# Hybrid token mixer on one core: state decay and scan products shared between VectorE and ScalarE, chunk norm column by column

## The chip, the core and the metric

The kernel runs on one core of a Trainium2 chip. A core has five engines that work side by side: TensorE (PE: matmuls, with weight loads listed as PEld), VectorE (DVE), ScalarE (ACT), GpSimd (POOL) and SyncE (SP, which here issues DMAs). Each engine works through its own instructions strictly in order, and waits for others by semaphores. SBUF is the on-chip memory that all of them read and write; PSUM receives TensorE's results.

The metric is device time in microseconds (us) of one execution. Before the change three runs took 1203.91, 1203.28 and 1203.84 us, with a median of 1203.84.

## The reference, cut to what matters

One layer: a token mixer with three parallel head groups (a state-space scan, SSD, in both directions; a Fourier mix; a pooling mix), whose outputs go through one output projection, and then a feed-forward part with a depthwise convolution. 1024 latent tokens of width 1024, and 256 context tokens from which the scan states start. The change lies in the scan and in the norm behind it:

```python
def ssd_chunked(X, dA, B, C, init_state):        # chunks of 128 tokens, 8 heads of 64 in 2 groups
    ...
    y_diag = jnp.einsum("bclhn,bcshn,bhcls,bcshp->bclhp", C, B, Lmat, X)
    decay_states = jnp.exp(A_cs[..., -1:] - A_cs)
    states = jnp.einsum("bclhn,bhcl,bclhp->bchpn", B, decay_states, X)
    ...
    new_states = jnp.einsum("bhzc,bchpn->bzhpn", chunk_decay, states)
    ...
    y_off = jnp.einsum("bclhn,bchpn,bhcl->bclhp", C, states, jnp.exp(A_cs))
    return (y_diag + y_off).reshape(b, L, h, p), final_state

def ssd_gate_norm(y, xs, z, d_skip, norm_w):
    y = (y + xs * d_skip[:, None]).reshape(bsz, L, SSD_WIDTH)
    y = (y * jax.nn.silu(z)).reshape(bsz, L, SSD_GROUPS, SSD_WIDTH // SSD_GROUPS)
    y = (y * lax.rsqrt(jnp.mean(y * y, -1, keepdims=True) + EPS)).reshape(bsz, L, SSD_WIDTH)
    return (y * norm_w).astype(z.dtype)
```

## The kernel before

The input projection leaves its columns in channel blocks; the last four of them are two Fourier blocks (pf0, pf1) and two pooling blocks (pp0, pp1). Each is a loop of 48 matmuls of 512 columns (`proj_feat`: 8 steps in the depth, each with weight block high and low part, as float32 products are made of rounded high and low halves). The scan is written as pieces (`mids`) into these loops, after every second step in depth, and runs while TensorE works on the projections.

**State steps.** `state_step(n, d)` carries the state of direction d (0 forward, 1 backward) over one chunk, seven steps each, 14 in all. GpSimd weights the chunk's inputs (`xweight`, L685, into `xw`, two buffers). Two matmuls (L710) leave the chunk's contribution in a PSUM tile `pst`. On VectorE L712 multiplies the old state (128 x 512: 2 groups x 4 heads x 64) with the decay of each head, `etot`, read by broadcast, and L715 adds `pst`; L717 writes the new state to DRAM. Steps 0 to 4 stand in the loop of pf1, steps 5 and 6 in that of pp0. In the same stretch stand the last masks of the scan (L645, L648 on ScalarE), the Fourier constants `cf` (L732/733, a DMA, and the matmuls pPQ, L738) and the Fourier fold of four blocks (L756 to L772).

**Scan chunks.** The chunks are taken in the order 4, 5, 6, 7, 3, 2, 1, 0. `Y(i)` calls the norm of the chunk before (`chunk_norm`), the products of the current one (`chunk_y`), and the transposes of the one before (`chunk_out`). In `chunk_y`:
- L900, GpSimd: y = skip x input, 128 x 512
- L908, TensorE: po = C x state, for each group a PSUM tile of 512 columns (2 directions x 4 heads x 64); L912: pd, eight products with the masks M
- L914, VectorE: t1 = po x `ecs` (one factor per row, direction and head, read by broadcast), one instruction of 128 x 512 per group. t1 has one buffer for all chunks
- L918: y += pd; L920, twice: y += one direction of t1; L921: y *= z, all on VectorE
- L924 to L928, ScalarE: the sum of squares of each group of 256, then Ln and Exp for a first reciprocal root

`chunk_norm` (L933 to L935) makes a Newton step on the two numbers of a row at once (`newton` with n = 2, four instructions, the last at L150) and multiplies y with the result by broadcast, 128 x 512. `chunk_out` transposes y in four blocks on TensorE (L940), and ScalarE copies them with a scale by column to yT (L944).

**Around them.** `wo_prep` loads a block of the output weights, multiplies it with the gate `g1b` (L975, on VectorE and GpSimd by turns) and splits it into a high part (L218, ScalarE) and a low part (L219). The first blocks' turns lie between the scan chunks; so do the pooling sums (L831 to L864) and the four-block Fourier products (L784, L787). Behind the scan stands the output projection (`out_tiles`, L1010).

**What sets the order.** The code is written stage by stage; a scheduler turns it into one instruction order for each engine, from its own costs of instructions and their dependencies. So an edit also moves instructions that it doesn't touch. Four PSUM tiles of 512 columns are shared in this stage by pst, pinit, po, pd, pyt and others.

## Time and profile before

| | |
|---|---|
| runs, median | 1203.91, 1203.28, 1203.84; 1203.84 us |
| profiled execution | 1204.77 us |
| its span | 1202.9 us |
| PE busy | 1129.9 us, 94% |
| PE weight loads | 918.1 us, 76% |
| DVE busy | 984.6 us, 82% |
| POOL busy | 609.5 us, 51% |
| ACT busy | 461.1 us, 38% |

The span runs from the first to the last instruction of the profiled execution; 1.9 us of its time lie around it. The shares are averages over stages with different limits: the input part up to some 230 us, the state steps and the scan chunks from about 241 to 398 us, and from there the output projection and the feed-forward part, which fill the rest. What the change touches lies in the middle stretch alone.

### The profile page before, as it was taken

To read this page: it belongs to the slowest core of one execution; us is meant where nothing else is said; L and a number is where in the kernel's file an instruction comes from. 1 tells how busy PE (TensorE), PEld (TensorE's weight loads), DVE (VectorE), ACT (ScalarE), POOL (GpSimd) and SP (SyncE) were. 2 spreads that over 40 slices of the span, in tenths; PEclk is the share of its full clock that TensorE was granted. 3 is DMA by queue.
4 is the path that set the end of the run, shared out by engine and by line. 5 is a ranking of instruction groups with operands and counts; after the bars stand their busy time and mean duration, and the time that the engine had idled before them with its cause. 6 is when DMAs were issued, how large, how long until landed. Compare 5 with 4: busy or idle time off the path is not lost.

```text
span 1202.9 us, 15202 instructions
## 1 busy us (share of the span) xinstructions
PE 1129.9 (94%) x5328; PEld 918.1 (76%) x5328; DVE 984.6 (82%) x1395; ACT 461.1 (38%) x790; POOL 609.5 (51%) x482
## 2 busy tenths in 40 slices
PE   4999999989878999899999999999999999999986
PEld 1698887777756787788888787888888888888864
DVE  4788787688899789799999968787777877777966
ACT  1273566721344232433232343333333334343553
POOL 0010122244254025664556477767676767676756
PEclk9999999999999999899999999999999999999988
DMA  9849465567524404223555346665556555555513
GB/s 309 283 163 324 128 213 167 170 195 221 189 89 166 148 35 141 97 88 108 172 166 176 118 154 219 192 199 175 182 183 190 193 192 190 188 184 184 197 40 140
DMA packets 151875, 206.48 MB, mean 172 GB/s; under 512 B 12253, under 2 KB 89067, under 8 KB 151799
## 3 DMA queue, kind: packets, MB, share of 16 engines
q1 hardware_dynamic: 151799, 205.51, 52.7%
q8 instruction: 42, 0.69, 0.2%
q14 instruction: 34, 0.28, 0.1%
HBM read 148.76 MB, written 56.71 MB: 171 GB/s over the span
## 4 chain that ended last, share of the span: by engine, by line
PE 69%; DVE 16%; DMA 6%; issue 3%; ACT 3%; POOL 2%; SPq 0%; DVEq 0%; ACTq 0%; POOLq 0%
PE pu L1353 22%; PE pdn L1187 16%; PE pu L1527 9%; PE pout L1010 4%; PE px L445 4%; PE pz L344 4%; PE pl L1584 3%; PE p L1353 3%; DMA bc<-cs_scratch 2%; DVE cv L1234 1%; PE pu L1245 1%; POOL cv L1224 1%; DMA xr<-in_x_dram 1%; DMA zb_r<-in_w_in_dram 1%; PE pm L298 1%
## 5 line engine op out<-in xcount | busy, mean ns | idle before, releaser
L1234 DVE SCALAR_TENSOR_TENSOR cv<-pu,ffc,cv 128x945 f32<-128x945 f32 (+6 forms) x362 | 425.6, 1180 | 74.1 <-ACT cv L1212 64.3
L1187 PE MATMUL pdn<-wd,gh 128*128 128x512 f32 x576 | 180.7, 395 | 0.3 <-DVE xt L1190 0.3
L1187 PEld LDWEIGHTS pdn<-wd,gh 128*128 128x128 f32 x576 | 108.2, 188 | 25.8 <-DVE xt L1190 1.0
L1187 PE MATMUL pdn<-wd,gl 128*128 128x512 f32 x288 | 113.6, 394 | 0.0
L1190 DVE TENSOR_TENSOR xt<-xt,pdn 128x512 f32<-128x512 f32 x128 | 87.4, 683 | 28.8 <-PE pdn L1187 24.4
L219 POOL TENSOR_TENSOR wul<-wur,wuh 128x1024 fp32r<-128x1024 f32 x29 | 72.3, 2495 | 39.3 <-ACT wuh L218 30.7
L1455 POOL TENSOR_TENSOR wdr<-wdr,g2b 128x512 f32<-128x512 f32 x44 | 57.4, 1309 | 54.7 <-DMA wdr<-in_ffn_w_down_dram 53.1
L219 POOL TENSOR_TENSOR S<-wur,S 128x384 fp32r<-128x384 f32 (+2 forms) x75 | 62.6, 861 | 36.8 <-ACT S L218 24.4
L1481 POOL TENSOR_TENSOR cv<-cv,cv 128x512 f32<-128x512 f32 x44 | 57.9, 1336 | 27.7 <-ACT cv L1480 27.7
L1212 ACT ACTIVATE cv<-pu,ffc 128x1024 f32<-128x1024 f32 (+3 forms) x46 | 53.4, 1164 | 43.5 <-PE pu L1353 21.5
L1353 PE MATMUL pu<-T,S 128*128 128x512 f32 x270 | 67.5, 393 | 0.4 <-POOL S L219 0.4
L644 POOL TENSOR_TENSOR bc<-bc,ncs 128x256 f32<-128x256 f32 x32 | 25.7, 807 | 76.4 <-DMA bc<-cs_scratch 62.1
L1187 PEld LDWEIGHTS pdn<-wd,gl 128*128 128x128 f32 x288 | 54.1, 188 | 12.8
L1480 ACT ACTIVATE cv<-cv 128x512 f32<-128x512 f32 x44 | 25.5, 625 | 90.9 <-DVE cv L1234 90.9
L1353 PEld LDWEIGHTS pu<-T,S 128*128 128x128 f32 x270 | 50.5, 188 | 12.8 <-POOL S L219 0.8
L1353 PE MATMUL pu<-h2h,wuh 128*128 128x512 f32 x150 | 59.1, 394 | 0.0
L206 POOL TENSOR_TENSOR h2l<-h2t,h2h 128x512 fp32r<-128x512 f32 x14 | 20.5, 1475 | 75.9 <-DVE h2h L205 75.9
L1353 PE MATMUL pu<-h2h,wul 128*128 128x512 f32 x150 | 59.0, 393 | 0.0
L1353 PE MATMUL pu<-h2l,wuh 128*128 128x512 f32 x150 | 58.5, 390 | 0.0
L219 POOL TENSOR_TENSOR gl<-cv,gh 128x512 fp32r<-128x512 f32 x44 | 56.7, 1309 | 1.5 <-PE pl L1584 0.7
L219 POOL TENSOR_TENSOR wd<-wdr,wd 128x512 fp32r<-128x512 f32 x42 | 53.8, 1303 | 4.7 <-ACT wd L218 4.6
L1527 PE MATMUL pu<-h2h,wuh 128*128 128x512 f32 x176 | 55.3, 395 | 0.0
(407 smaller groups left out, 2939.6 us busy)
## 6 DMA issues: line engine op xcount, KB each, us to landing
xt<-x_scratch SPq DMA_DIRECT2D x144, 256.0 KB
x_scratch<-xt SPq DMA_DIRECT2D x144, 256.0 KB
wur<-in_ffn_w_up_dram SPq DMA_DIRECT2D x44, 512.0 KB
wad<-in_w_ada_dram SPq DMA_DIRECT2D x32, 512.0 KB
wdr<-in_ffn_w_down_dram SPq DMA_DIRECT2D x44, 256.0 KB
wa<-in_w_ada_dram SPq DMA_DIRECT2D x32, 256.0 KB
bc<-cs_scratch SPq DMA_DIRECT2D x32, 256.0 KB
xr<-in_x_dram SPq DMA_DIRECT2D x8, 512.0 KB
```

Source lines behind the costliest of these rows:

```text
L219: return (eng or G).tensor_tensor(lo, raw, hi.bitcast(F32), op=ALU.subtract)
L344: TE.matmul(pt[:, j * 512 : j * 512 + ZW], a, b[:, k % 4, :], start=first and i == 0, stop=last and i == 2)
L445: TE.matmul(pt[:, q * 512 : q * 512 + 512], a[:, k, :], b[q][:, k, :], start=k == 0 and i == 0, stop=k == KD - 1 and i == 2)
L1010: TE.matmul(pt[:, nb * 512 : nb * 512 + 512], u, v[:, nb * 512 : nb * 512 + 512], start=first and i == 0, stop=last and i == 2)
L1187: TE.matmul(pt, u_, wd[nb][:, v_, :], start=i == 0, stop=i == n - 1)
L1190: V.tensor_tensor(xt, xt, pt, op=ALU.add)
L1212: tap[0] = S.activation(acc[:, a * 64 : b * 64], pt[:, a * 64 : b * 64], AF.Identity, bias=ffc[:, 396 + ct : 397 + ct], scale=factor(0, 0))
L1234: last = V.scalar_tensor_tensor(dst, pv[:, r0 + dy : r1 + dy, c0 + dx : c1 + dx], factor(dy, dx), dst, op0=ALU.mult, op1=ALU.add)
L1353: TE.matmul(dst, a[k][u], b[k][w], start=start and k == 0 and j == 0, stop=k == n - 1 and j == 2, skip_group_check=True)
L1455: G.tensor_tensor(raw, raw, g2b[:, s], op=ALU.mult)
L1481: G.tensor_tensor(acc[:, s], acc[:, s], acc_v[:, s], op=ALU.mult)
L1527: TE.matmul(pt[:, q * 512 : q * 512 + 512], a[:, k, :], b[q][:, k, :], start=k == 0 and j == 0, stop=k == KD - 1 and j == 2)
```

## The change

Three edits, all within the scan. What is computed stays the same.

- **Decay of the state.** The multiply of 128 x 512 on VectorE becomes one of 128 x 256 (group one); group two is done by four ScalarE instructions of 128 x 64, one for each head, with the factor of that head as a scale by row. The addition (now L717) waits for both.
- **Scan products.** Of the two multiplies of 128 x 512 in each chunk the second (group two) is replaced by eight ScalarE instructions of 128 x 64, one for each direction and head, that read po in PSUM and write t1. The additions (now L923) wait for both.
- **Chunk norm.** The Newton step is made for each of the two columns by itself (`newton` with n = 1, three instructions with a scalar by row, L141, L142, L144), and the multiply of 128 x 512 by broadcast becomes two of 128 x 256 with a scalar by row (L939).

GpSimd's sums of the blocks of h, and all else that GpSimd does, are the same before and after.

```diff
--- before.py
+++ after.py
@@ -709,9 +709,11 @@
         for g in range(2):
             TE.matmul(pt[:, g * 256 : g * 256 + 256], btok[g][:, ch, :], xw[:, g, :], start=True, stop=True)
         dst, src = qt(stag[d](), f"st{d}_{n + 1}", [P, 2, 256]), state[d]
-        V.tensor_tensor(dst[:].rearrange("p g (h q) -> p g h q", q=64),
-                                      src[:].rearrange("p g (h q) -> p g h q", q=64),
-                                      dv(etot, ch, d).unsqueeze(3).broadcast_to([P, 2, 4, 64]), op=ALU.mult)
+        V.tensor_tensor(dst[:, 0].rearrange("p (h q) -> p h q", q=64), src[:, 0].rearrange("p (h q) -> p h q", q=64),
+                        dv(etot, ch, d)[:, 0].unsqueeze(2).broadcast_to([P, 4, 64]), op=ALU.mult)
+        for h in range(4):
+            S.activation(dst[:, 1, h * 64 : h * 64 + 64], src[:, 1, h * 64 : h * 64 + 64], AF.Identity,
+                         scale=etot[:, ch, 8 + 4 * d + h : 9 + 4 * d + h])
         V.tensor_tensor(dst, dst, pt[:].rearrange("p (g n) -> p g n", g=2), op=ALU.add)
         state[d] = dst
         nc.sync.dma_start(ss[ch + 1 - 2 * d][:, d, :], dst[:].rearrange("p g n -> p (g n)"))
@@ -910,10 +912,11 @@
         pd = psb(f"pd{ch}")
         for i in range(8):
             TE.matmul(pd[:, i * 64 : i * 64 + 64], M[:, i, :], xt[:, i * 64 : i * 64 + 64], start=True, stop=True)
-        for g in range(2):
-            V.tensor_tensor(t1[:, g].rearrange("p d (h q) -> p (d h) q", q=64),
-                            pos[g][:].rearrange("p (a q) -> p a q", q=64),
-                            ecs[:, ch, g * 8 : g * 8 + 8].unsqueeze(2).broadcast_to([P, 8, 64]), op=ALU.mult)
+        V.tensor_tensor(t1[:, 0].rearrange("p d (h q) -> p (d h) q", q=64), pos[0][:].rearrange("p (a q) -> p a q", q=64),
+                        ecs[:, ch, 0:8].unsqueeze(2).broadcast_to([P, 8, 64]), op=ALU.mult)
+        for a in range(8):
+            S.activation(t1[:, 1, a // 4, (a % 4) * 64 : (a % 4) * 64 + 64], pos[1][:, a * 64 : a * 64 + 64], AF.Identity,
+                         scale=ecs[:, ch, 8 + a : 9 + a])
         yv = y[:].rearrange("p (g n) -> p g n", g=2)
         V.tensor_tensor(y, y, pd, op=ALU.add)
         for d in range(2):
@@ -931,8 +934,9 @@
     def chunk_norm(ch, y, yv, ssq, r):
         v = sm.tile([P, 2], F32, tag="sv", name=f"sv{ch}")
         V.tensor_scalar(v, ssq, 1.0 / 256.0, EPS, op0=ALU.mult, op1=ALU.add)
-        r = newton(r, v, 2, f"ssn{ch}")
-        V.tensor_tensor(yv, yv, r.unsqueeze(2).broadcast_to([P, 2, 256]), op=ALU.mult)
+        for g in range(2):
+            q = newton(r[:, g : g + 1], v[:, g : g + 1], 1, f"ssn{ch}{g}")
+            V.tensor_scalar(yv[:, g], yv[:, g], q, None, op0=ALU.mult)
 
     def chunk_out(ch, y, *_):
         py = psb(f"pyt{ch}")
```

Lines behind the edits shift by two to four: L715 becomes L717, L918 L921, L920 L923, L921 L924, L940 L944, L975 L979. ScalarE has 14 x 4 + 8 x 8 = 120 instructions more; VectorE has eight products fewer, and three instructions more in each of the eight norms. The order of the feed-forward part does not change. At three places it does in the stretch between.

**ScalarE, state steps.** st0_n and st1_n are the states of the two directions after n steps, pinit the first one, EU and bc parts of the scan's masks, wp0 and wp1 the weight blocks of pp0 and pp1, fu0 a copy of Fourier block pf0. Before:

```order
L645 ACTIVATE EU11_2429<-bc112_2436,ncs_1072 128x128 x2
L218 ACTIVATE wp0_h_2485<-wp0_r_2483 128x1024
L648 ACTIVATE EU11_2429<-EU11_2429 128x512
L752 COPY fu0_2463<-pf0_2308 128x512
L701 COPY st1_0_2419<-pinit1_2410 128x512
L645 ACTIVATE EU01_2551<-bc010_2552,ncs_1072 128x128 x2
L645 ACTIVATE EU01_2551<-bc012_2558,ncs_1072 128x128 x2
L648 ACTIVATE EU01_2551<-EU01_2551 128x512
L218 ACTIVATE wp1_h_2685<-wp1_r_2683 128x1024
```

After, from the same first state of direction 1:

```order
L701 COPY st1_0_2419<-pinit1_2410 128x512
L715 ACTIVATE st1_1_2463<-st1_0_2419,etot_1070 128x64 x4
L715 ACTIVATE st0_2_2527<-st0_1_2450,etot_1070 128x64 x4
L715 ACTIVATE st1_2_2540<-st1_1_2463,etot_1070 128x64 x4
L645 ACTIVATE EU01_2567<-bc010_2568,ncs_1072 128x128 x2
L645 ACTIVATE EU01_2567<-bc012_2574,ncs_1072 128x128 x2
L715 ACTIVATE st0_3_2588<-st0_2_2527,etot_1070 128x64 x2
L648 ACTIVATE EU01_2567<-EU01_2567 128x512
L715 ACTIVATE st0_3_2588<-st0_2_2527,etot_1070 128x64 x2
L715 ACTIVATE st0_4_2644<-st0_3_2588,etot_1070 128x64 x4
L715 ACTIVATE st1_3_2601<-st1_2_2540,etot_1070 128x64 x4
L218 ACTIVATE wp1_h_2725<-wp1_r_2723 128x1024
```

The decays of steps 1 to 4 now stand between the first state and the high part of wp1; the masks EU01 stand between those of steps 2 and 3, and the masks EU11, the high part of wp0 and the copy fu0 ahead of the first row shown.

**VectorE, from the last state step to the first scan chunk.** t1, po, pd, y and z are the tiles of chunk_y with the chunk's number; wor0 is the first block of output weights and g1b its gate. Before:

```order
L712 TENSOR_TENSOR st0_7_2737<-st0_6_2707,etot_1070 128x512
L712 TENSOR_TENSOR st1_7_2746<-st1_6_2716,etot_1070 128x512
L715 TENSOR_TENSOR st0_7_2737<-st0_7_2737,pst0_6_2734 128x512
L715 TENSOR_TENSOR st1_7_2746<-st1_7_2746,pst1_1_2743 128x512
L975 TENSOR_TENSOR wor0_3077<-wor0_3077,g1b_3075 128x1024
L914 TENSOR_TENSOR t1_4_2764<-po40_2765,ecs_1071 128x512
L914 TENSOR_TENSOR t1_4_2764<-po41_2768,ecs_1071 128x512
L918 TENSOR_TENSOR y4_2762<-y4_2762,pd4_2771 128x512
L920 TENSOR_TENSOR y4_2762<-y4_2762,t1_4_2764 128x512 x2
L918 TENSOR_TENSOR y5_2807<-y5_2807,pd5_2816 128x512
L921 TENSOR_TENSOR y4_2762<-y4_2762,z4_2655 128x512
```

After:

```order
L712 TENSOR_TENSOR st0_7_2785<-st0_6_2747,etot_1070 128x256
L712 TENSOR_TENSOR st1_7_2798<-st1_6_2760,etot_1070 128x256
L717 TENSOR_TENSOR st0_7_2785<-st0_7_2785,pst0_6_2782 128x512
L717 TENSOR_TENSOR st1_7_2798<-st1_7_2798,pst1_1_2795 128x512
L915 TENSOR_TENSOR t1_4_2820<-po40_2821,ecs_1071 128x512
L979 TENSOR_TENSOR wor0_3176<-wor0_3176,g1b_3174 128x1024
L921 TENSOR_TENSOR y4_2818<-y4_2818,pd4_2827 128x512
L923 TENSOR_TENSOR y4_2818<-y4_2818,t1_4_2820 128x512 x2
L924 TENSOR_TENSOR y4_2818<-y4_2818,z4_2695 128x512
```

The two decays are half as wide. One product of chunk 4 remains, and it stands ahead of the multiply of the weight block by the gate, no longer behind it; the chain of chunk 4 then runs through to the multiply by z, and the first addition of chunk 5 no longer stands in it.

**TensorE, where chunk 4 is transposed.** pp1 is the last pooling block, hl and hh the halves of the modulated input, pyt the transposed chunk, pft and pex the Fourier products, po60 and po61 the products of chunk 6. Before, after 34 of the 48 matmuls of pp1:

```order
L445 MATMUL pp1_2891<-hl0_193,wp1_h_2685 128x512
L445 MATMUL pp1_2891<-hl1_194,wp1_h_2685 128x512
L940 MATMUL pyt4_2837<-ident_75,y4_2762 128x128 x4
L784 MATMUL pft00_2870<-PQW_2585,f40_2469 128x128 x4
L784 MATMUL pft01_2876<-PQW_2585,f40_2469 128x128 x4
L787 MATMUL pex0_2882<-fex0_2478,PQW_2585 128x2
L908 MATMUL po60_2928<-S6_2794,cT6_1341 128x256 x2
L908 MATMUL po61_2931<-S6_2794,cT7_1540 128x256 x2
```

After, behind 8 of the 48:

```order
L445 MATMUL pp1_2966<-hh0_191,wp1_h_2725 128x512
L445 MATMUL pp1_2966<-hh1_192,wp1_h_2725 128x512
L944 MATMUL pyt4_2912<-ident_75,y4_2818 128x128 x2
L786 MATMUL pft00_2945<-PQW_2609,f40_2477 128x128 x4
L786 MATMUL pft01_2951<-PQW_2609,f40_2477 128x128
L944 MATMUL pyt4_2912<-ident_75,y4_2818 128x128 x2
L786 MATMUL pft01_2951<-PQW_2609,f40_2477 128x128 x3
L789 MATMUL pex0_2957<-fex0_2486,PQW_2609 128x2
L445 MATMUL pp1_2966<-hl0_193,wp1_h_2725 128x512
L445 MATMUL pp1_2966<-hl1_194,wp1_h_2725 128x512
```

The transposes of chunk 4 have moved ahead by 26 matmuls of pp1, and the Fourier products pft stand around them; those of chunk 6 have moved ahead by 10, behind the 24th.

On SP the DMA of the Fourier constants now stands ahead of the two state writes of step 2, the load of wor0 behind the state writes of step 1, and that of g1b between the two of step 7. On VectorE the low part of wp0 (L219) stood ahead of the first additions and now stands behind them, inside the Fourier fold (ahead of L773).

## Rows read from the trace of the kernel before

**Rows 1.** Busy time by stage, core 0; x counts instructions.

```profile
core 0: us, PE busy (x) PEld busy (x) DVE busy (x) ACT busy (x) POOL busy (x), PEclk, DMA share, GB/s
241.00:286.00 45.00, 39.90 (x172) 32.47 (x171) 41.65 (x79) 7.49 (x16) 24.93 (x23) 0.96 0.64 202
286.00:388.00 102.00, 83.34 (x427) 68.15 (x427) 90.28 (x143) 38.35 (x97) 41.20 (x20) 0.94 0.49 157
388.00:439.00 51.00, 51.00 (x219) 40.82 (x218) 39.30 (x99) 11.40 (x27) 0.00 (x0) 0.98 0.33 123
```

**Rows 2.** Waits of PE, 240 to 286 us: total us, times, longest.

```profile
PE pst L710 <- POOL xw L685: 2.6, 3, 1.1
PE pPQ L738 <- DMA cf<-in_fnet_w_dram: 2.5, 1, 2.5
```

**Rows 3.** Waits of PE, 286 to 390 us, the same columns.

```profile
PE pyt L940 <- DVE y L935: 6.2, 3, 3.0
PE ppool L871 <- DVE pT L864: 3.8, 1, 3.8
PE pyt L940 <- DVE s L863: 2.3, 1, 2.3
...
PE po L908 <- DVE t L914: 0.9, 1, 0.9
```

**Rows 4.** Groups of VectorE by shape, whole run: busy, mean ns | idle before.

```profile
L712 DVE TENSOR_TENSOR st<-st,etot 128x512 f32<-128x512 f32 x14 | 12.2, 882 | 0.1
...
L914 DVE TENSOR_TENSOR t<-po,ecs 128x512 f32<-128x512 f32 x16 | 10.5, 682 | 1.1 <-PE po L908 1.0
...
L150 DVE TENSOR_TENSOR ssn_q<-sr,ssn_t 128x2 f32<-128x2 f32 x8 | 6.7, 834 | 0.2
...
L320 DVE TENSOR_SCALAR xr<-xr,ln_mv,ln_q 128x1024 f32<-128x1024 f32 x6 | 4.6, 806 | 0.0
...
L141 DVE TENSOR_SCALAR pn_t<-pn_r,pn_v 128x1 f32<-128x1 f32 x16 | 4.3, 266 | 0.3
```

**Rows 5.** Timeline of VectorE: start, us, instruction, [idle before].

```profile
289.42 1.23 DVE L975 TENSOR_TENSOR wor<-wor,g1b 128x1024 f32<-128x1024 f32 x1 [3.40 <-DMA g1b<-ada_scratch]
290.57 1.28 DVE L914 TENSOR_TENSOR t<-po,ecs 128x512 f32<-128x512 f32 x2
...
292.48 0.94 DVE L920 TENSOR_TENSOR y<-y,t 128x512 f32<-128x512 f32 x1
...
302.84 2.32 DVE L150 TENSOR_TENSOR ssn_q<-sr,ssn_t 128x2 f32<-128x2 f32 x1
...
447.76 0.27 DVE L141 TENSOR_SCALAR pn_t<-pn_r,pn_v 128x1 f32<-128x1 f32 x1
...
448.26 0.21 DVE L144 TENSOR_SCALAR pn_q<-pn_t,pn_r 128x1 f32<-128x1 f32 x1
```

**Rows 6.** Group of ScalarE by shape, whole run.

```profile
L944 ACT ACTIVATE yT<-pyt,col 128x128 f32<-128x128 f32 x32 | 9.3, 367 | 22.8 <-PE pyt L940 22.8
```

**Rows 7.** Timeline of ScalarE in the scan stage.

```profile
296.62 1.06 ACT L218 ACTIVATE woh<-wor 128x1024 fp32r<-128x1024 f32 x1
...
297.77 0.99 ACT L831 COPY pT<-pp 128x1024 f32<-128x1024 f32 x1
...
307.82 1.14 ACT L944 ACTIVATE yT<-pyt,col 128x128 f32<-128x128 f32 x4 [4.87 <-PE pyt L940]
```

**Rows 8.** Timeline of TensorE, chunk 4.

```profile
287.55 1.90 PE L912 MATMUL pd<-xt,M 128*128 128x64 f32 x16
289.28 1.08 PE L908 MATMUL po<-S,cT 128*128 128x256 f32 x4
```

**Rows 9.** Timeline of GpSimd, three places.

```profile
289.53 3.33 POOL L975 TENSOR_TENSOR wor<-wor,g1b 128x1024 f32<-128x1024 f32 x1 [3.80 <-DMA g1b<-ada_scratch]
...
302.75 2.39 POOL L975 TENSOR_TENSOR wor<-wor,g1b 128x1024 f32<-128x1024 f32 x1 [9.89 <-DMA wor<-in_w_out_dram]
...
447.40 2.85 POOL L206 TENSOR_TENSOR h2l<-h2t,h2h 128x512 fp32r<-128x512 f32 x2 [1.50 <-DVE h2h L205]
```

## The prediction

> **What bounds the kernel now.** I looked first for the stretch in which the touched lines run (L712 from 241.9 us, L914 and L935 up to 398 us) and cut the run into stages there [rows 1]. From 241 to 286 us TensorE works 39.9 of 45 us, from 286 to 388 us only 83.3 of 102, and from 388 to 439 us all 51. So in the stage of the scan chunks TensorE stands idle 18.7 us, in the stage of the state steps 5.1 us, and behind 388 us it is the bound again. VectorE is busy 90.3 of 102 us and 41.7 of 45, ScalarE 38.4 and 7.5. A gain ahead of 388 us is kept behind it: the output projection runs without a gap, and the order of the feed-forward part does not change. Then I asked what ended TensorE's waits. In the state steps they are GpSimd's weighted inputs (2.6 us in three waits) and one DMA, that of the Fourier constants (2.5 us) [rows 2]. In the scan stage VectorE ends most [rows 3]: y of L935 6.2 us, pT 3.8, s 2.3 (this is the same wait for y, put down to its neighbour), t of L914 0.9. The kinds left out there end mostly on ScalarE and GpSimd. So 13.2 of the 18.7 us of idle end on VectorE. This is a stage bound by VectorE's chain from chunk to chunk, with ScalarE free for more than half of it.
>
> **Decay of the state (L712).** 14 multiplies of 128x512, 882 ns each on average [rows 4], become 128x256. An unhindered 512-wide one takes 0.68 us (L914), a 1024-wide one 1.23 (the first of [rows 5]), so 256 columns are worth 0.55 / 2 = 0.275 us: 14 x 0.275 = **3.9 us of VectorE**. Four ScalarE pieces of 128x64 with a scale by column replace them. The nearest row is L944, the same form at 128 columns out of PSUM: 0.367 us, four in 1.14, a pace of 0.26 [rows 6, 7]. Less 64 columns at 0.77 ns (from 0.367 at 128 columns to 1.06 at 1024 in the same rows) that is 0.32 us and a pace of 0.21; four take 0.95 us, 56 some 12 to 14 us. ScalarE has 37 us free there. What is new is a wait: L715 cannot add before ScalarE's four pieces, and on ScalarE the decays of step 4 stand behind the copy of wp1, which waits for TensorE. Behind a late L715 on VectorE wait the next steps and the fold; TensorE would wait if the PSUM tiles of pst came free late, and those are four steps ahead.
> Moved with it: the copy of wp0's low part leaves the place ahead of the first additions on VectorE, and on SP the Fourier constants go ahead of two state writes. Their DMA is issued once VectorE has merged the last masks, so a shorter VectorE chain brings it earlier. The most that can come of this stage is its 5.1 us of idle; the least is nothing, since 2.6 us end on GpSimd. Nothing says that all of either side is right, so I take half: **-2.5 us** (bounds 0 and -5.1; a loss is the second rival).
>
> **Scan products (L914).** Eight of 16 leave VectorE, each 0.60 us at its pace (two in 1.28, one 0.68 [rows 4, 5]): 8 x 0.60 = 4.8 us. Eight pieces on ScalarE per chunk take 0.32 + 7 x 0.21 = 1.8 us; they start when the product po of group two is done, and the products pd, which L918 needs first, then take another 1.73 us (1.90 with the overlap [rows 8]). So ScalarE's part is hidden as long as it starts at once. Not all 4.8 us are on the path. At 290.57 both L914 run while a GpSimd multiply is under way (289.53 to 292.86), and the sum L920 behind them, which reads SBUF twice, ends only 0.56 us after it [rows 5, 9]: one L914 less there gives nothing. By the timeline the second L914 of chunks 4, 7, 3 and 2 lies so beside GpSimd or ahead of a wait for TensorE or ScalarE, that of chunk 6 ahead of pd, that of chunk 0 behind 388 us. In the old order only chunks 5 and 1 gain: 1.2 us. In the new order VectorE has the first L914 ahead of the multiply that waits for g1b, and y4 is not woven into the pool sums any more, so more of it should count. Between 1.2 and 4.8 I take **-2.5 us**.
> The Trainium skill ("SBUF — State Buffer", section "Who interferes with whom") says that a VectorE instruction with two SBUF inputs contends with a GpSimd one that reads SBUF, and one with at most one SBUF input outside the two-port modes does not. Here the trace agrees (L914 ran on, L920 and L150 waited), and by that rule the products now moved held nothing that GpSimd wants; what it would make of the time is the first rival.
>
> **Norm by columns (L935).** One 128x512 multiply (0.68 us unhindered, as L914) becomes two of 128x256 with a scalar by row. TENSOR_SCALAR takes 0.27 us at one column (L141) and 0.81 at 1024 (L320), so 0.40 at 256 [rows 4]: two are 0.7 to 0.8 us. The Newton step goes from four small instructions to six, at most 2 x 0.2 us more: 8 x (0.1 + 0.4) = 4 us dearer at worst. Against it: L150 costs 6.7 us for eight results of two numbers [rows 4], since it waits for GpSimd (2.32 us at 302.84, ending with GpSimd's multiply [rows 5, 9]), whereas one-column steps run beside GpSimd (the three of 447.76 to 448.47 inside GpSimd's 447.40 to 450.25 [rows 5, 9]). The wait only moves to the multiply behind it, but the four or six steps are then done. I take **-0.5 us** (bounds +4 and -5).
>
> **The sum.** The profiled run took 1204.77 us, 0.93 above the median of 1203.84. -2.5 - 2.5 - 0.5 = -5.5 us, so 1199.3 in its own terms and **1198.3** by the median. TensorE's clock, granted at 0.94 and 0.96 in these stages against 0.98 behind them [rows 1], may give a little more where its waits go; I count it at nought.
>
> **Rivals.** *The shared reading of SBUF is the bound.* VectorE's two-input steps and GpSimd's steps exclude one another, and GpSimd is busy 41 of the 102 us [rows 1]. The moved products are not among those steps. Then stage one, whose waits end on GpSimd and a DMA, gives nothing, the scan stage the 1.2 us that the old order shows: 1204.77 - 1.2 - 0.93 = 1202.6, no change that can be measured. For it speaks [rows 5, 9]; against it that L712 is such a step and is halved, and L150 loses its wait.
> *ScalarE becomes the chain.* It works in order. In the scan stage the pieces of t stand in one queue with the copies of w_out (1.06 us) and pT (0.99 us) [rows 7]; if a chunk's pieces come behind both, they end 1.8 + 2.05 + 0.1 = 3.95 us after po instead of within pd's 1.73, so L920 starts 2.2 us late, once per chunk. Five of TensorE's waits end on a chunk's y or t: 5 x 2.2 = +11 us, with the -5.5 that makes 1203.84 + 5.5 = 1209.3. The single buffer of t1 adds to it: ScalarE can't write the next chunk's pieces until VectorE has read this one's. It decides once the delay exceeds 5.5 / 5 = 1.1 us per chunk. Against it: ScalarE is idle 64 of 102 us, and in the new order most groups of eight pieces stand ahead of the copies.
> *The whole chain comes loose.* y4 is transposed after 8 of the 48 products of pp1 instead of 34, so the waits of 2.3, 6.2 and 0.9 us in [rows 3] could go altogether, with the 2.5 us of the constants: -11.9 + 0.5, about 1192. Against it: TensorE now meets y4 earlier, and a late y4 stops it there with 40 products still to do.
>
> **How the numbers follow.** The forecast with its neighbourhood, 1195 to 1201.4: 0.40. The chain comes loose, below 1195: 0.17. SBUF is the bound, within 0.2% (1201.4 to 1206.2, about what a measurement of this kernel can tell from no change): 0.24. ScalarE is the chain, above 1206.2: 0.19. So faster 0.57, same 0.24, slower 0.19. The range goes from 1191, which cuts off perhaps 0.08 at the low end (the bounds -5.1 - 4.8 together with a gain in the norm), to 1207, half-way into the slower case, which leaves out about 0.12.
>
> **What would show it.** Right: TensorE idle in the state stage below 5 us, with its wait for the constants shorter, and in the scan stage below 16 us; the pieces at 0.3 us each; no wait of VectorE on ScalarE ahead of L920 or L715 longer than 0.5 us; the small steps of the norm without stalls of 2 us. Wrong: VectorE idle ahead of L920 or L715 for ScalarE (second rival); VectorE as long as before in steps of two SBUF inputs, with the stalls moved onto L935 and L920 (first rival); new waits of TensorE at the transposes of y, which now stand earlier. A difference behind 450 us would mean that the shift is not passed on, which I exclude here.

## The result and the profile after

Four runs of the changed kernel took 1195.23, 1194.09, 1193.51 and 1196.94 us, with a median of 1194.66; the kernel before has 1203.88 over four runs. The ratio is 0.9926 (95% interval 0.9909 to 0.9944): **8.9 us less, between 6.7 and 11.0**. The forecast was 1198.3, 5.5 less. The profiled execution took 1195.23 us, with a span of 1193.5.

The stages of [rows 1], after (the same columns):

```profile
241.00:286.00 45.00, 42.19 (x197) 34.31 (x196) 36.76 (x80) 23.53 (x79) 22.01 (x22) 1.00 0.66 217
286.00:388.00 102.00, 87.20 (x433) 71.97 (x432) 87.20 (x171) 53.79 (x168) 42.93 (x20) 0.92 0.51 175
388.00:439.00 51.00, 51.00 (x237) 41.10 (x236) 39.70 (x95) 13.12 (x26) 2.58 (x2) 1.00 0.21 76
```

TensorE idles 2.8 us where it idled 5.1, and 14.8 where it idled 18.7. VectorE is busy 4.9 and 3.1 us less, ScalarE 16.0 and 15.4 us more. The windows are the same clock times, but the changed kernel is up to some 4 us further on in its work; the stages further down are cut by the work instead. The waits of TensorE, from 240 to 286 us and from 286 to 390 us:

```profile
PE pst L710 <- POOL xw L685: 1.2, 2, 0.9
PE pst L710 <- DVE st L717: 0.9, 1, 0.9
PE pPQ L740 <- DMA cf<-in_fnet_w_dram: 0.6, 1, 0.6
```
```profile
PE ppool L873 <- DVE pT L866: 4.9, 1, 4.9
PE pyt L944 <- DVE y L939: 4.1, 2, 2.1
PE pyt L944 <- DVE ssn_q L144: 3.3, 1, 3.3
PE pout L1014 <- POOL yl L219: 1.6, 1, 1.6
PE po L910 <- ACT ft L787: 0.9, 1, 0.9
```

Against [rows 2] the wait for the Fourier constants fell from 2.5 to 0.6. Against [rows 3] the waits that end on y moved rather than went: one of 3.3 us now stands where chunk 4 is transposed. The groups of VectorE and ScalarE that the edits touch (form, count | busy, mean ns | idle before), to be laid beside [rows 4] and [rows 6]:

```profile
L923 DVE TENSOR_TENSOR y<-y,t 128x512 f32<-128x512 f32 x16 | 17.0, 1063 | 0.9
...
L712 DVE TENSOR_TENSOR st<-st,etot 128x256 f32<-128x256 f32 x14 | 8.3, 605 | 0.1
L939 DVE TENSOR_SCALAR y<-y,ssn_q 128x256 f32<-128x256 f32 x16 | 8.1, 532 | 0.0
...
L915 DVE TENSOR_TENSOR t<-po,ecs 128x512 f32<-128x512 f32 x8 | 5.5, 686 | 1.7 <-PE po L910 1.7
...
L141 DVE TENSOR_SCALAR ssn_t<-sr,sv 128x1 f32<-128x1 f32 x16 | 3.7, 267 | 1.2 <-ACT sr L931 1.2
...
L144 DVE TENSOR_SCALAR ssn_q<-ssn_t,sr 128x1 f32<-128x1 f32 x16 | 2.9, 207 | 0.0
...
L142 DVE TENSOR_SCALAR ssn_t<-ssn_t 128x1 f32<-128x1 f32 x16 | 2.2, 146 | 0.0
```
```profile
L715 ACT ACTIVATE st<-st,etot 128x64 f32<-128x64 f32 x56 | 15.0, 336 | 11.3 <-DVE st L717 10.3 <-DMA s_scratch<-st 0.6 <-DMA m_scratch<-EU 0.4
L918 ACT ACTIVATE t<-po,ecs 128x64 f32<-128x64 f32 x64 | 14.5, 328 | 18.2 <-PE po L910 9.6 <-DVE y L923 8.7
```

The sums of t (L923, before the change L920) were shorter before:

```profile
L920 DVE TENSOR_TENSOR y<-y,t 128x512 f32<-128x512 f32 x16 | 14.2, 889 | 0.3
```

**A ruler for all runs.** From TensorE's timeline I took four marks in each profile: the first matmul of the initial states, the first scan product, the products of the second pooling block (ppool, 359.49 us before), and the first matmul of the up-projection. Between them lie the state stage, the scan up to the pool, and the rest of the scan with the output projection. What follows the last mark took 735 to 738 us in every kernel, before and after alike; nothing was lost or won there. What lies ahead of the first mark took 235.6 to 239.9 us, though no edit touches it: that is how far one profile scatters.

| kernel | ratio of the times (95%) | state | to the pool | on to up | sum |
|---|---|---|---|---|---|
| before | 1 | 47.0 | 73.7 | 107.2 | 227.9 |
| all three edits | 0.9926 (0.9909 to 0.9944) | 43.5 | 69.5 | 107.4 | 220.4 |
| decay alone | 0.9982 (0.9968 to 0.9995) | 44.0 | 74.4 | 106.0 | 224.5 |
| products alone | 0.9949 (0.9931 to 0.9968) | 47.6 | 66.6 | 106.7 | 220.9 |
| norm alone | 0.9933 (0.9918 to 0.9949) | 45.5 | 69.1 | 104.0 | 218.7 |
| products and norm | 0.9951 (0.9935 to 0.9967) | 47.9 | 65.5 | 107.4 | 220.9 |
| decay and norm | 0.9935 (0.9912 to 0.9958) | 43.7 | 70.5 | 104.1 | 218.3 |
| order alone | 1.0004 (0.9990 to 1.0019) | 47.5 | 72.2 | 107.6 | 227.4 |
| products and norm, old order | 0.9983 (0.9969 to 0.9998) | 48.2 | 72.0 | 107.3 | 227.5 |
| all three, gate multiply later | 0.9945 (0.9924 to 0.9966) | 44.0 | 68.5 | 109.0 | 221.4 |
| before, gate multiply later | 0.9979 (0.9963 to 0.9994) | 47.1 | 67.6 | 107.6 | 222.3 |
| before, GpSimd's gate out | 0.9922 (0.9899 to 0.9945) | 47.4 | 70.0 | 101.2 | 218.6 |
| all three, GpSimd's gate out | 0.9879 (0.9855 to 0.9903) | 43.7 | 65.3 | 103.5 | 212.4 |
| all three, products' pieces twice | 0.9961 (0.9945 to 0.9976) | 44.5 | 73.8 | 104.9 | 223.2 |

The ratios are medians of 4 to 12 runs against before on the same chip; the stages are one profile each. Single executions of before went from 1196.7 to 1207.0 us in these comparisons, so a stage of one profile can be off by a few us and the ratios lead. The expectations quoted below count the stages a little otherwise (from the initial state of the second direction, 42.48 to 39.01 us; to the transposes behind the post-norm, 154.71 to 150.66, or 132.3 to 128.2 counted to the first of them); the differences, 3.5 and 4.05 us, are the same.

### The profile page after: what moved, and what is told of

Read it like the earlier page. It is cut to its first block, busy times and chain, and to the rows that moved or that the text cites. A ratio compares the mean times of both kernels' runs of the same rounds, so it can differ in the third digit from the quotient of the medians.

```text
span 1193.5 us, 15370 instructions
## 1 busy us (share of the span) xinstructions
PE 1125.1 (94%) x5328; PEld 914.8 (77%) x5328; DVE 971.3 (81%) x1411; ACT 488.9 (41%) x910; POOL 608.4 (51%) x482
## 4 chain that ended last, share of the span: by engine, by line
PE 55%; DVE 12%; DMA 4%; issue 3%; POOL 3%; ACT 1%; SPq 0%; DVEq 0%; ACTq 0%; POOLq 0%
PE pu L1357 21%; PE pdn L1191 14%; PE pu L1531 5%; PE pout L1014 4%; PE pl L1588 3%; PE p L1357 2%; DMA x_scratch<-xt 2%; DVE cv L1238 2%; PE pp L445 2%; PE pu L1249 1%; POOL cv L1228 1%; DVE y L923 1%; DVE xt L1194 1%; DVE T L219 1%; DVE xa L1084 1%
## 5 line engine op out<-in xcount | busy, mean ns | idle before, releaser
L219 POOL TENSOR_TENSOR wul<-wur,wuh 128x1024 fp32r<-128x1024 f32 x29 | 72.3, 2495 | 39.7 <-ACT wuh L218 39.7
L219 POOL TENSOR_TENSOR S<-wur,S 128x384 fp32r<-128x384 f32 (+2 forms) x75 | 62.1, 855 | 32.2 <-ACT S L218 24.3
L219 POOL TENSOR_TENSOR gl<-cv,gh 128x512 fp32r<-128x512 f32 x44 | 56.8, 1311 | 1.5 <-PE pl L1588 0.7
L219 POOL TENSOR_TENSOR wd<-wdr,wd 128x512 fp32r<-128x512 f32 x42 | 53.8, 1302 | 4.4 <-ACT wd L218 4.4
```

The costliest lines, as they stand in the source:

```text
L219: return (eng or G).tensor_tensor(lo, raw, hi.bitcast(F32), op=ALU.subtract)
```

## The experiments

### Each edit alone, and two together

The decay alone:

```diff
-        V.tensor_tensor(dst[:].rearrange(...), src[:].rearrange(...), ..., op=ALU.mult)
+        V.tensor_tensor(dst[:, 0].rearrange(...), src[:, 0].rearrange(...), ..., op=ALU.mult)
+        for h in range(4):
+            S.activation(dst[:, 1, ...], src[:, 1, ...], AF.Identity, scale=etot[...])
```

> Only the first edit: group two of the state's decay on ScalarE, scan products and norm as before. In the traces the stage from the first matmul of the initial states (L698) to the first scan product (L908) shrank from 42.48 to 39.01 us, the stage from there to the first transposes behind the post-norm (L189) from 154.71 to 150.66. Theory A, the parts act each in its own stage: the first stage is 3.5 us shorter here (39.0), the second one as before (154.7 within 0.5), the time 3.0 to 4.0 us below before. Theory B, the first stage gained only because the Fourier constants were issued earlier on SP (they stand ahead of the writes of step 2 here too): TensorE's wait for them falls from 2.5 to 0.6 us and its other waits in the stage stay as they were, so the gain is 2.0 us. Theory C, two-input reads of SBUF beside GpSimd are the bound: under 1 us.

Measured: 0.9982, 2.2 us less (0.6 to 3.8); the state stage 3.0 us shorter, the scan as before. TensorE's waits from 240 to 286 us:

```profile
PE pst L710 <- POOL xw L685: 2.0, 2, 1.6
PE pPQ L740 <- DMA cf<-in_fnet_w_dram: 0.8, 1, 0.8
PE pst L710 <- DVE st L717: 0.4, 1, 0.4
```

The wait for the constants gives 1.7 us, near the 1.9 of theory B, and the idle of the stage falls by as much (5.1 to 3.4 us). The other part of the 3.0 is TensorE's clock. In the profile of before the granted clock fell to the lower of its two levels, 1.2 instead of 2.4 GHz, behind the wait for the constants (windows of 3 us; PEclk is the third figure from the end):

```profile
260.00:263.00 3.00, 1.18 (x6) 0.70 (x4) 3.00 (x7) 0.63 (x1) 2.54 (x2) 1.00 0.96 234
263.00:266.00 3.00, 2.29 (x10) 2.22 (x11) 1.87 (x6) 0.00 (x0) 0.12 (x1) 0.64 0.63 238
266.00:269.00 3.00, 3.00 (x12) 2.40 (x11) 2.80 (x6) 0.20 (x1) 0.00 (x0) 0.79 0.32 87
```

0.36 and 0.21 of 3 us are 1.7 us, some of it while TensorE was idle; the matmuls of the whole stage were busy 41.9 us before and 40.7 with the decay on ScalarE, where the clock stays at 1.00. That is 1.3 us of the 3.0. The other profiles bear it out: in the six kernels with the new decay TensorE waited 0.6 to 0.9 us for the constants and the clock of the stage is 1.00; in seven of the eight with the old one it waited 2.5 to 3.5 us and the clock of the stage is 0.93 to 0.96. The eighth shows that the clock doesn't fall behind each such wait: with the norm alone TensorE waited 2.6 us at the same place and the clock stayed up (state stage 45.5).

The products alone:

```diff
-        for g in range(2):
-            V.tensor_tensor(t1[:, g]..., pos[g]..., ecs[...], op=ALU.mult)
+        V.tensor_tensor(t1[:, 0]..., pos[0]..., ecs[...], op=ALU.mult)
+        for a in range(8):
+            S.activation(t1[:, 1, ...], pos[1][...], AF.Identity, scale=ecs[...])
```

> Only the second edit: group two of the scan products on ScalarE; decay and norm as before. The transposes of chunk 4 stand after 13 of 48 matmuls of the last pooling block here (34 before, 8 with all three edits), the products of chunk 6 after 24 (34 before). Theory A, VectorE's chain is shorter by what leaves it: the stage from the first scan product to the post-norm transposes is 2.5 us shorter, and the time too; the other stage is as before. Theory B, the shared reading of SBUF is the bound, and the products are not among the steps that suffer from it: 1.2 us at most. Theory C, ScalarE's pieces come late: no gain or a loss, with VectorE waiting for ScalarE ahead of the additions of t. Theory D, it is the new order of TensorE that counts (chunk 6 is started 10 matmuls earlier): as much as with the norm alone, which has the same place for chunk 6.

Measured: 0.9949, 6.1 us less; all of it (7.0 us) between the first scan product and the pool. That is more than twice theory A's 2.5, and speaks against B and C. Seen from TensorE, 3.9 of the 7.0 us are less idle and 3.2 are shorter matmuls: its clock, 0.95 in this stretch before, is 0.98 here (the table under "What the waits for GpSimd cost").

The norm alone:

```diff
-        r = newton(r, v, 2, f"ssn{ch}")
-        V.tensor_tensor(yv, yv, r.unsqueeze(2).broadcast_to([P, 2, 256]), op=ALU.mult)
+        for g in range(2):
+            q = newton(r[:, g : g + 1], v[:, g : g + 1], 1, f"ssn{ch}{g}")
+            V.tensor_scalar(yv[:, g], yv[:, g], q, None, op0=ALU.mult)
```

> Only the third edit: the norm by columns; decay and products as before. The transposes of chunk 4 stand after 23 of 48 matmuls of the last pooling block, the products of chunk 6 after 24. Theory A (the prediction's term): 0.5 us less, bounds 5 less and 4 more; L150's 6.7 us are gone, but the wait has moved to the multiply behind it. Theory D, the order counts (chunk 6 started 10 matmuls earlier): as much as the products alone, 2 us or more.

Measured: 0.9933, 8.1 us less, as much as all three edits and far from theory A's 0.5. (Of the 9.2 us by which the stages of its profile are shorter, 1.5 lie in the state stage, which this edit doesn't touch.) Of before, L150 stands in [rows 4] with 6.7 us; its neighbours in the Newton step were not cheap either:

```profile
L146 DVE TENSOR_TENSOR ssn_t<-sr 128x2 f32<-128x2 f32 x8 | 3.4, 426 | 1.1 <-ACT sr L928 1.0
L147 DVE TENSOR_TENSOR ssn_t<-ssn_t,sv 128x2 f32<-128x2 f32 x8 | 2.9, 368 | 0.1
L148 DVE TENSOR_SCALAR ssn_t<-ssn_t 128x2 f32<-128x2 f32 x8 | 2.5, 309 | 0.1
```

Together the four took 6.7 + 3.4 + 2.9 + 2.5 = 15.5 us. With the norm alone:

```profile
L936 DVE TENSOR_SCALAR y<-y,ssn_q 128x256 f32<-128x256 f32 x16 | 11.6, 738 | 0.1
...
L141 DVE TENSOR_SCALAR ssn_t<-sr,sv 128x1 f32<-128x1 f32 x16 | 3.7, 265 | 0.8 <-ACT sr L928 0.8
L144 DVE TENSOR_SCALAR ssn_q<-ssn_t,sr 128x1 f32<-128x1 f32 x16 | 3.0, 205 | 0.0
...
L142 DVE TENSOR_SCALAR ssn_t<-ssn_t 128x1 f32<-128x1 f32 x16 | 2.2, 144 | 0.0
```

The six steps take 8.9 us in all eight chunks. The multiply rose from 7.6 us (L935 before, whole run) to 11.6: part of the wait did move there, but 6.6 went and 4.0 came. These 2.6 us alone don't make 8.1. Besides, y now becomes ready in halves: two of chunk 4's four transposes and the Fourier products run before the second half is there. What the halves are worth by themselves was not tested.

Products and norm together:

> Second and third edit together, the decay as before. The transposes of chunk 4 stand after 8 of 48 matmuls, as with all three edits. Theory A, the stages are independent: the first stage as before (42.5 us), the second as with all three (150.7), the time 4.0 us below before, and this gain and that of the decay alone add up to that of all three (9.2 by the medians, of which 1.6 lie ahead of and behind both stages in the traces and may not repeat). Theory D, the order makes the gain: no more than the better of the products alone and the norm alone.

Measured: 0.9951, 5.9 us less and no more than either alone. These two gains don't add up. The first stage is as before, and the stretch to the pool 65.5 us, not the 69.5 of all three edits as theory A has it. By the medians the decay's 2.2 us and these 5.9 do come to 8.1 of the 8.9 of all three; in the profiles the decay's gain is gone at the pool (state stage and stretch together 113.4 us here, 113.0 with all three). Theory D, that TensorE's new order makes the gain, fits so far: in all three kernels chunk 6 begins ten matmuls earlier than before.

Decay and norm, the products by the old code, completes the set:

> Decay and norm by the new code, the products by the old. Alone the decay gave 0.18% and the norm 0.67%, all three 0.74%. Theory P (parts add up): 0.85%, 10 us below before, faster than all three. Theory E (what the state stage gains ends at the gate's DMA, for which VectorE waits ahead of chunk 4's sums): VectorE's wait for it is 3.5 to 4 us instead of 3.0, the scan stage is 2 to 3 us longer than the 124.6 of the norm alone, and the time is that of the norm alone, 0.6 to 0.75%.

Measured: 0.9935, 7.8 us less, the time of the norm alone, as theory E has it; the interval just takes in the 0.9915 of theory P, so the time alone doesn't exclude that the parts add up. VectorE waits for the gate ahead of chunk 4's sums, a little less than the 3.5 to 4 us expected, and the scan stage is 1.4 us longer than with the norm alone (126.0), not 2 to 3:

```profile
286.96 1.23 DVE L978 TENSOR_TENSOR wor<-wor,g1b 128x1024 f32<-128x1024 f32 x1 [3.35 <-DMA g1b<-ada_scratch]
```

### Order without work, work without order

The kernel before, with the matmuls of pp1 behind the 24th issued behind the transposes of chunk 5:

```diff
+                    with tc.issue_after(anchor[0].ins) if anchor[0] is not None else ExitStack():
                         TE.matmul(pt[:, q * 512 : q * 512 + 512], a[:, k, :], b[q][:, k, :], ...)
...
-    p1 = proj_p(1, wnext, [[], [Y(2)], [], [Y(3)]])
+    p1 = proj_p(1, wnext, [[], [Y(2), hold], [], [Y(3)]])      # hold: anchor[0] = last transpose
```

> The kernel before with none of the three edits; only TensorE's order is changed: the matmuls of the last pooling block behind its 24th are issued behind the transposes of chunk 5, so that chunk 4 is transposed after 24 of them and chunk 6 begins there (34 and 34 before). The scan stage, counted here from the first scan product to the first transposes behind the post-norm, took 132.3 us before, 124.7 with the products alone, 124.6 with the norm alone, 124.3 with both, 128.2 with all three edits. Theory D, the place of chunk 6 in TensorE's order is what shortened it: 124 to 126 us here, the time 6 to 8 us below before. Theory A, the work that left VectorE shortened it: no gain, since VectorE has all of it here; the transposes of chunk 4 wait 2 to 4 us longer, 132 us or more.

Measured: 1.0004, no gain. Theory D, that the order alone does it, falls: TensorE meets chunk 4 earlier, and waits for it (its waits from 286 to 390 us; the wait is put down to a neighbour of y in VectorE's queue):

```profile
PE ppool L875 <- DVE pT L868: 5.6, 1, 5.6
PE pyt L944 <- DVE s L867: 4.5, 1, 4.5
```

Products and norm, with chunk 4's transposes, the first Fourier products and chunk 6 held behind the 36th matmul:

```diff
-    four_chan(0, *f0)
...
-    p1 = proj_p(1, wnext, [[], [Y(2)], [], [Y(3)]])
+    p1 = proj_p(1, wnext, [[], [], [out4, Y(2)], [Y(3)]])      # out4: chunk_out(4), four_chan(0)
```

> Products and norm by the new code, decay by the old one, but TensorE's order held near that of before: chunk 4 is transposed, the first Fourier products are made and chunk 6 begins behind the 36th of 48 matmuls of the last pooling block (34 before; with the same two edits and the scheduler's own order 8 and 24). Theory D (order): the gain is lost, the scan stage is 131 to 133 us (before 132.3, the same two edits in their own order 124.3). Theory A (work that left VectorE): most of the gain stays, 127 us or less.

Measured: 0.9983, 2.0 us of the 5.9. So neither theory holds by itself: less work on VectorE is worth 2 us while TensorE keeps its old order, the new order is worth nothing while VectorE has its old work, and together they are worth some 6.

### The gate's DMA ahead of chunk 4

With all three edits VectorE's timeline reads (start, us, instruction, [idle before]):

```profile
282.83 0.69 DVE L915 TENSOR_TENSOR t<-po,ecs 128x512 f32<-128x512 f32 x1 [0.55 <-PE po L910]
287.21 1.22 DVE L979 TENSOR_TENSOR wor<-wor,g1b 128x1024 f32<-128x1024 f32 x1 [3.69 <-DMA g1b<-ada_scratch]
288.35 0.68 DVE L921 TENSOR_TENSOR y<-y,pd 128x512 f32<-128x512 f32 x1
289.14 2.90 DVE L923 TENSOR_TENSOR y<-y,t 128x512 f32<-128x512 f32 x2
```

The scan stage begins 4.05 us earlier than before (281.77 against 285.82), but the gate lands only 2.2 us earlier (287.21 against 289.42, [rows 5]), and VectorE stands still for it with chunk 4's products waiting. TensorE then waits, and its clock falls behind the wait (the transposes of chunk 4; windows of 3 us):

```profile
296.91 0.45 PE L944 MATMUL pyt<-ident,y 128*128 128x128 f32 x1 [3.32 <-DVE ssn_q L144]
```
```profile
293.00:296.00 3.00, 0.58 (x3) 0.15 (x1) 3.00 (x11) 3.00 (x13) 0.00 (x0) 0.99 0.28 86
296.00:299.00 3.00, 2.09 (x10) 2.12 (x11) 2.97 (x6) 2.09 (x7) 0.00 (x0) 0.50 0.15 16
299.00:302.00 3.00, 3.00 (x15) 2.96 (x14) 1.13 (x6) 2.29 (x6) 1.04 (x1) 0.50 0.22 76
302.00:305.00 3.00, 3.00 (x13) 2.42 (x12) 3.00 (x12) 0.03 (x1) 0.00 (x0) 0.87 0.01 3
```

The lower level takes up to (0.50 + 0.50 + 0.13) x 3 = 3.4 us there. The kernel before loses as much elsewhere in this stretch (granted clock 0.95 in both), the products and the norm without the decay next to nothing (0.99): the same matmuls are busy 58.7 us with all three edits and 56.6 with those two. Would it help to issue that multiply behind chunk 4?

```diff
+        with tc.issue_after(gated[4].ins) if i == 0 else ExitStack():      # gated[4]: y4 *= z4
-        (G if i % 2 else V).tensor_tensor(raw, raw, g1b[0], op=ALU.mult)
+            (G if i % 2 else V).tensor_tensor(raw, raw, g1b[0], op=ALU.mult)
```

> All three edits; on VectorE the multiply of the first output weight block by the gate is issued behind chunk 4's multiply by z, no longer ahead of its additions. With all three edits VectorE waits 3.69 us there for the gate's DMA, chunk 4 is transposed late (TensorE waits 3.3 us) and the granted clock is at half for some 6 us behind it. Theory E, this wait eats what the state's decay gained: the wait at the transposes of chunk 4 goes, the clock does not fall there, the scan stage is 122 to 125 us instead of 128.2 and the time 4 to 6 us below that of all three edits (1194.7). Theory F, the decay's ScalarE pieces or the DMAs are what costs the 4 us: the stage stays at 127 to 129.

> The kernel before with none of the three edits; on VectorE the multiply of the first output weight block by the gate (3.40 us of wait for the gate's DMA ahead of it) is issued behind chunk 4's multiply by z. The scheduler then transposes chunk 4 after 18 of 48 matmuls of the last pooling block and begins chunk 6 after 24. Theory D (order): a scan stage of 123 to 126 us and a time 6 to 9 us below before, as the products or the norm alone bring. Theory A (work that left VectorE): only the wait counts, 1 to 3 us below before.

Measured: 0.9945 with all three edits (not better than 0.9926, the intervals overlap) and 0.9979 without them, 2.5 us less, which is A's 1 to 3 and not D's 6 to 9. With all three edits the first half of theory E came true: chunk 4 is transposed 13.5 us behind the first scan product instead of 15.1, TensorE's wait there is 1.2 us instead of 3.3, the clock doesn't fall behind it, and chunk 6 begins 19.2 us behind the first scan product instead of 24.1. The second half didn't: the scan stage takes 128.8 us, a length that theory F had named, though VectorE doesn't wait for ScalarE's pieces in this trace. VectorE's sums of chunk 4 (L923) now start at 284.10 and take 3.54 us, because GpSimd's multiply by the gate begins beside them. VectorE's and GpSimd's timelines, and the group of the pooling results:

```profile
284.10 3.54 DVE L923 TENSOR_TENSOR y<-y,t 128x512 f32<-128x512 f32 x2
```
```profile
284.74 2.35 POOL L980 TENSOR_TENSOR wor<-wor,g1b 128x1024 f32<-128x1024 f32 x1 [6.43 <-DMA g1b<-ada_scratch]
```
```profile
L862 DVE SCALAR_TENSOR_TENSOR pT<-s,pe,pT 64x1008 f32<-64x1008 f32 x4 | 9.1, 2284 | 0.1
```

Those four took 5.0 us before (1259 ns each) and 7.0 with all three edits (1761), and TensorE's wait for the second pooling block is 6.6 us instead of 4.9. VectorE's stalls beside GpSimd up to that place grew by 3.6 us (11.3 to 14.9, the table below), about as much as the 3.7 us saved at the gate.

### What the waits for GpSimd cost

To see their price, GpSimd's four multiplies by the gate were left out (10.9 us of GpSimd in the trace of before; those weight blocks are then not gated), before and after:

```diff
-        (G if i % 2 else V).tensor_tensor(raw, raw, g1b[0], op=ALU.mult)
+        if i % 2 == 0:
+            V.tensor_tensor(raw, raw, g1b[0], op=ALU.mult)
```

> The kernel before, but the four multiplies of an output weight block by the gate that are GpSimd's are left out (those blocks are not gated). Two of them lie in the stretch from the first scan product to the products of the second pooling block (73.7 us before, 69.1 with the norm alone, 69.5 with all three edits), 3.33 and 2.39 us long; VectorE's result of two numbers (L150) took 2.32 us beside the second. TensorE's order stays. Theory G (VectorE's steps that read SBUF twice wait for GpSimd, and the chain passes that on): L150 takes under 0.3 us at that place, chunk 4 is transposed some 2 us earlier, the stretch is 2 to 4 us shorter. Theory N (the stalls lie beside other waits): the stretch is as long within 1 us.

> All three edits, GpSimd's four multiplies by the gate left out as in the other kernel of this kind. With all three edits the sums of t (L923) took 2.90 us for two beside the first multiply and 2.75 beside the second, 1.3 us unhindered. Theory G: they take 1.3 to 1.6 us there, chunk 4 is transposed 1.5 us earlier, TensorE's wait of 3.3 us shrinks by as much, and the stretch to the products of the second pooling block is 2 to 4 us shorter than 69.5. Theory N: within 1 us of it.

Measured: 0.9922 and 0.9879, that is 9.4 us below before, and some 5.7 below all three edits (0.9926 - 0.9879, two comparisons). VectorE at the two places (the first line without the edits, where [rows 5] has 2.32 us; the second with them, where 2.90 stood):

```profile
300.20 0.16 DVE L150 TENSOR_TENSOR ssn_q<-sr,ssn_t 128x2 f32<-128x2 f32 x1
```
```profile
288.76 1.49 DVE L923 TENSOR_TENSOR y<-y,t 128x512 f32<-128x512 f32 x2
```

Theory G holds: the stretch to the pool is 3.7 and 4.2 us shorter with TensorE's order unchanged, chunk 4 is transposed 2.9 and 1.5 us earlier. That much is shown. With all three edits 2.7 of the 4.2 us are busy time of TensorE (58.7 to 56.1): it waits 1.8 us for chunk 4 instead of 3.3, and its clock stays at 1.00 throughout. Not all of the 9.4 us need be contention: without the multiply the weight blocks are also ready sooner for the splits and the output projection, which gained 6.0 us; the two weren't separated.

For the whole stretch the stalls can be counted from VectorE's timeline. For each instruction from the first scan product to the pool I took its time less the shortest that the same operation and shape took there in any of these runs, where that is over 0.15 us. Every instruction so counted overlaps one of GpSimd. Beside it stands TensorE in the same stretch (one profile each; us, and the granted clock):

| kernel | stretch | TensorE busy | TensorE idle | clock | VectorE's stalls |
|---|---|---|---|---|---|
| before | 73.7 | 59.9 | 13.8 | 0.95 | 15.0 |
| decay alone | 74.4 | 61.1 | 13.4 | 0.93 | 15.6 |
| products alone | 66.6 | 56.7 | 9.9 | 0.98 | 11.9 |
| norm alone | 69.1 | 56.8 | 12.3 | 0.96 | 11.8 |
| products and norm | 65.5 | 56.6 | 9.0 | 0.99 | 12.2 |
| decay and norm | 70.5 | 56.9 | 13.7 | 0.99 | 12.0 |
| all three edits | 69.5 | 58.7 | 10.7 | 0.95 | 11.3 |
| order alone | 72.2 | 59.2 | 13.1 | 0.94 | 10.7 |
| products and norm, old order | 72.0 | 60.5 | 11.5 | 0.92 | 17.0 |
| all three, gate multiply later | 68.5 | 57.9 | 10.5 | 0.95 | 14.9 |
| before, GpSimd's gate out | 69.9 | 61.1 | 8.9 | 0.93 | 13.1 |
| all three, GpSimd's gate out | 65.3 | 56.1 | 9.2 | 1.00 | 7.9 |

TensorE does the same matmuls in every row; what differs in its busy time comes with its clock. The products and the norm each take some 3 us of stalls out, and together no more than one of them. The stalls alone don't rank the kernels: with the order alone they are 10.7 us, yet the stretch is nearly as long as before.

### Is ScalarE near its limit?

```diff
         for a in range(8):
-            S.activation(t1[:, 1, ...], pos[1][...], AF.Identity, scale=ecs[...])
+            for _ in range(2):
+                S.activation(t1[:, 1, ...], pos[1][...], AF.Identity, scale=ecs[...])
```

> All three edits, each of the 64 pieces of the scan products on ScalarE issued twice (the same result written again): 1.7 us more on ScalarE per chunk, 14 us in all. The scheduler then transposes chunk 4 after 10 matmuls of the last pooling block instead of 8. The rival of the prediction (ScalarE becomes the chain): a chunk's sum comes 1.7 us later where the pieces aren't covered by pd, in five chunks or more, 8 us and more on the time. The prediction (hidden behind pd as long as ScalarE is free for it): 8 pieces took 1.75 us beside a pd of 1.9, 16 end 1.6 us behind it; ScalarE's queue is otherwise empty there, so up to 1.6 us in the two or three chunks at which TensorE waits for y, 0 to 5 us in all.

Measured: 0.9961, some 4.2 us above all three edits. ScalarE in chunk 4, and its group:

```profile
284.96 4.51 ACT L919 ACTIVATE t<-po,ecs 128x64 f32<-128x64 f32 x16 [2.54 <-PE po L910]
```
```profile
L919 ACT ACTIVATE t<-po,ecs 128x64 f32<-128x64 f32 x128 | 34.9, 321 | 7.9 <-DVE y L924 3.9 <-PE po L910 2.9
```

Even 64 pieces too many, 20 us more busy time than the 14.5 above, cost no more than the prediction's own reading allows and half of what the rival asks. ScalarE isn't the chain.

## Why the prediction came out as it did

The sign and the range were right, 1194.7 within 1191 to 1207; the size was 5.5 us against 8.9. Step by step:

- **What bounds the stretch** was right: VectorE's chain from chunk to chunk. Behind 388 us the gain is kept, as claimed.
- **The decay, -2.5 us (0 to -5.1):** right. Alone it gave 2.2 us by the medians and 3.0 in the stage. VectorE's 3.9 us came as worked out (12.2 to 8.3), the pieces took 0.336 us against 0.32, the stage idles under 5 us and the constants are waited for 0.6 us. "I count it at nought", of the clock, was wrong in this stage: 1.3 us of the 3.0 are a fall of the clock that no longer happens.
- **The products, -2.5 us (1.2 to 4.8):** mis-sized; alone they gave 6.1. The work fell as worked out (10.5 to 5.5 us, forecast 4.8 less), ScalarE's eight pieces are hidden (VectorE never waits for them ahead of a sum). The step that failed is the claim that of the second L914 only what is not beside GpSimd can count. The stalls were taken as fixed in place, but the shorter chain meets GpSimd's instructions elsewhere: 3.1 us of them went (15.0 to 11.9). And the clock was counted at nought here too: 3.2 of the 7.0 us by which the stretch is shorter are matmuls that ran faster.
- **The norm, -0.5 us (+4 to -5):** this term failed, at two places. It priced the four steps at their unhindered time and only L150 with its wait; they took 15.5 us, and the six take 8.8. And "the wait only moves to the multiply behind it" is half true: 6.6 us went, 4.0 came back on the multiply when the norm was alone, 0.5 with all three edits (8.1 against 7.6). Alone the norm gave 8.1 us, more than these steps of VectorE account for; the rest is argued from TensorE's new order and y in halves, and was not taken apart.
- **The sum** failed as well: the terms were added. Measured alone they are 2.2 + 6.1 + 8.1 = 16.4 us, together 8.9; norm and products together give no more than one of them. So the forecast came near by two errors of opposite sign, terms too small and a sum that isn't one. It is the norm and the products that don't add up: each takes some 3 us out of the same stalls (15.0 us before, 11.9 and 11.8 with one of them), together no more (12.2), and each alone already brings the new place of chunk 6. Whether that is all that limits them to the same 6 to 8 us stays open. For the decay it isn't settled. Its gain adds nothing to the norm's (0.9935 against 0.9933) but 3.0 us to that of products and norm (0.9951 to 0.9926, intervals that overlap); in the profiles the gain is gone by the pool, where VectorE stands at the gate's DMA, which follows the state stage by only half, and where TensorE's clock falls behind its wait for chunk 4.
- **"SBUF is the bound"**: its mechanism is there and large (leaving out 10.9 us of GpSimd's multiplies saves 9.4 us, though not all of it need be contention), and its sign was seen in part (the sums of t took 17.0 us against 14.2); its conclusion was wrong. It held that moving steps which never wait for GpSimd changes nothing; yet they stand in one queue with those that do, and shift them.
- **"ScalarE becomes the chain"** was wrong. The longest wait of VectorE on ScalarE ahead of a sum is 0.56 us (ahead of L717), a little over the 0.5 named.
- **"The whole chain comes loose"**, some 1192: the time came 2.7 us short of it, but its waits didn't go. The counter-argument given there was seen: TensorE meets y4 earlier and stops for 3.3 us, and the clock falls behind the stop.

The two levels of the measurement must be kept apart: the stages of the two profiles account for 7.5 of the 8.9 us; the rest is within what single executions scatter.

## What to carry to other kernels

Where an engine's chain is bound by stalls against another engine, price an instruction by its group's mean, stalls included, and look at all of its neighbours, not only the worst row: small steps of 150 ns cost 300 to 800 here. Edits that shorten one chain need not add up; measure each alone and in pairs before crediting any. A shorter chain and the scheduler's new order around it can each be worth little alone. Count TensorE's clock as a term of its own: the same matmuls took 56 to 61 us here by where its waits fell. And a wait that is removed from one chain (the gate's DMA) can come back as a collision with the engine beside it.

## What the runs showed of the hardware

Not only steps with two SBUF inputs were held up. The multiply by a scalar by row, which reads one tensor, took 2.72 us for two of 128x256 beside a GpSimd instruction (the first fence is VectorE with all three edits, the second GpSimd at the same time, the third VectorE with GpSimd's gate out):

```profile
316.26 2.72 DVE L939 TENSOR_SCALAR y<-y,ssn_q 128x256 f32<-128x256 f32 x2
```
```profile
316.44 2.38 POOL L219 TENSOR_TENSOR wol<-wor,woh 128x1024 fp32r<-128x1024 f32 x1 [3.86 <-ACT woh L218]
```
```profile
311.20 0.61 DVE L939 TENSOR_SCALAR y<-y,ssn_q 128x256 f32<-128x256 f32 x2
```

Another TENSOR_SCALAR, the step of the norm that forms 1.5 - 0.5 x t, averaged 309 ns on two columns (L148, before) and 146 on one (L142, with all three edits). The two-column form took up to 1048 ns beside GpSimd; the one-column form took 154 at most, though four of its 16 ran beside GpSimd. The Trainium skill ("SBUF — State Buffer", section "Who interferes with whom") says that tensor_scalar can enter modes that take both of VectorE's port pairs, and then blocks with GpSimd; the traces agree for the forms of 2 and 256 columns, and the prediction had applied only the half of the rule that speaks of two inputs. GpSimd's instructions stretch too: a split of 128x1024 took 4.49 us at 333.22 with all three edits, beside two-input sums of VectorE, and 2.4 at 316.44 and 324.93.
